# Layer 1 of a two-layer diffusion backbone: VectorE and ScalarE in program order, V projected two token tiles to a PSUM bank, output transposes of two tiles in one PSUM unit

## The chip, the core and the metric

The kernel runs on one core of one Trainium2 chip. A core has five engines with an instruction queue each: TensorE (PE: matmuls and transposes; PEld is its weight load), VectorE (DVE), ScalarE (ACT), GpSimd (POOL) and SyncE (SP, which issues DMA transfers). The metric is the time of the whole program on the device in microseconds. Lower is better.

## The reference

Two layers run over 1024 latent tokens of width 1024 and 256 context tokens. Layer 0 is multi-head latent attention, layer 1 differential attention. Both end in a gated output projection, a residual sum and a layer norm. The change touches layer 1 alone. It has 8 heads; a head has two query and two key maps of width 64 and one value of width 128:

```python
q, k, v, gate = jnp.split(t @ w_in, 4, axis=-1)
q, k = apply_rope(q, cos, sin), apply_rope(k, cos, sin)      # latent tokens only
o1 = softmax(q[..., 0] @ k_all[..., 0] * scale) @ v_all      # keys: latent and context tokens
o2 = softmax(q[..., 1] @ k_all[..., 1] * scale) @ v_all
o = rms_norm(o1 - lam_full * o2, g_sub) * (1.0 - lambda_init)
x = layer_norm(ALPHA * x + gate_x * ((o * silu(gate)) @ out_w), ln_g, ln_b)
```

The context stream of layer 1 is needed for its keys and values only, since layer 1 is the last.

## The kernel before

Activations of layer 1 lie transposed in SBUF as two fp16 halves, h1H and h1L (high part and rest), for 10 tiles of 128 tokens: tiles 0 to 7 latent, 8 and 9 context. Each product is three matmuls, high by high, low by high and high by low (`mm3`, L184 to L187). Splitting a value costs one ScalarE operation for the high part and one VectorE operation for the rest (`split`, `split16`, L175 to L182).

PSUM in layer 1 has two units of three banks (tag `s`, 1536 numbers a partition) for attention and two single banks (tag `b`) for projections. A new tile takes a buffer whose last user has been read; the instruction that writes first waits for that reader.

Attention of head h and token tile t is a step of `step1`, written out in TensorE's order:

- scores of map 0 into a unit (6 matmuls); on VectorE the row maximum (L1151), on ScalarE the exponential (L1152)
- a slot of side work, 3400 units of cost (`SLOT1`; a matmul of 512 columns costs 512)
- values of tile t-2 (30 matmuls, L1173 to L1175) and scores of map 1, both into the other unit; maximum and exponential; on ScalarE the copy of the values' result and its squares (L1179, L1180)
- a slot of 4300
- ten transposes of tile t-1 (L1167) into the unit that held scores 0, and their split into ph (ScalarE, L181) and pl (VectorE, L182)
- a slot of 6800
- on VectorE the combine of the two maps of tile t (L1154 to L1156)

The side work of head h is the projection of head h+1: K in chunks of 512, 512 and 256 tokens (`prod_k1`), Q in two of 512 (`prod_q1`), each with a rope on VectorE (L1048, L1049) and GpSimd (L1050, L1051), then V and the gate (`prod_v1`): the 256 context tokens transposed, then one bank for each token tile, emptied by ScalarE copies into Vf and gg (L1122, L1124). `prod_w` prepares a head's weights in stages: load, two squares (L979), a small matmul for the norm (L982) with its scale on VectorE and GpSimd, and two splits. `weave` starts its stages at the numbers of main yields in `WAT`. Closing work of K, Q and V (splits, the gate's SiLU with two table loads) is kept in `later` and run at the end of a step.

`tc.manual_schedule(engines=...)` names the engines whose instructions keep the program's order. In both layers that is TensorE (`MAN = 'P'`, `MAN1 = 'P'`). The order on the others is chosen by the framework's scheduler. `HP` sets its priority and is 0.

Head 7 has no projection beside it. `out_open` loads the rest of out_w (four weights, L1213, scaled by L1215, split by L176 and L177); from step 2 on the side work is the output projection of tile t-2 (`out_tile1`), with transposes by `out_turn`: seven blocks of the next tile in one unit, woven in by `out_turns`, and the tile's own last block in another, since head 7 gives it late (L1256).

Of the kernel before, what the change touches and what calls it, by code (L numbers as in the profile page):

```python
# [17 lines left out]
P = 128  # L18
D = 1024
KT = D // P  # L20
SEQ = 1024
# [10 lines left out]
H1, HD = 8, 64  # L32
LAMBDA_INIT = 0.8 - 0.6 * math.exp(-0.3 * 1)
PB = (3, 4)
WAT = ((6, 14, 21, 27, 34), (3, 10, 18, 25, 32))
NOW = 4
MAN = 'P'
MAN1 = 'P'
HP = 0
LAG = 2  # L40
CHUNKS = ((0, 512), (512, 512), (1024, 256))
# [12 lines left out]
def hybrid_kernel(  # L54
# [95 lines left out]
    idn = fv(idr)  # L150
# [132 lines left out]
    def pow2_of(scale, unscale, amax, target, g):  # L283
        dve.tensor_scalar(g[:, 0:1].bitcast(I32), amax.bitcast(I32), 0x7F800000, None, op0=ALU.bitwise_and)
        dve.reciprocal(g[:, 1:2], g[:, 0:1])
        dve.tensor_scalar_mul(scale, g[:, 1:2], target)
        dve.tensor_scalar_mul(unscale, g[:, 0:1], 1.0 / target)
# [669 lines left out]
    def w1(tag):  # L957
        sh, d, b = TAG1[tag]
        return rot(place[tag], sh, d, tag, b)
# [8 lines left out]
    def prod_w(h, which, bank_=lambda: bank("b"), load=sp):  # L968


        wt[which] = []
        ws, sq = [], w1("sq")
        for q in range(2):
            ws.append(w1("ws"))
            load.dma_start(ws[q], dw[q * 512:(q + 1) * 512, h, which * 256:(which + 1) * 256].rearrange(
                "(k p) c -> p k c", p=P))
        yield 0
        for q in range(2):
            act.activation(w1("wsq"), ws[q].rearrange("p a b -> p (a b)"), AF.Square, accum_out=sq[:, q:q + 1])  # L979
        yield 0  # L980
        bk = bank_()
        pe.matmul(bk[:, :2], ones, sq, start=True, stop=True)  # L982
        u, p2 = w1("uw"), w1("uw")
        dve.tensor_reduce(u[:, 0:1], bk[:, :2], axis=AX.X, op=ALU.add)
        pool.tensor_scalar(u[:, 0:1], u[:, 0:1], 1.01, 1e-30, op0=ALU.mult, op1=ALU.add)
        pool.tensor_tensor(u[:, 0:1], u[:, 0:1], poshalf, op=ALU.pow)
        pow2_of(u[:, 1:2], u[:, 0:1], u[:, 0:1], 16384.0, p2)

        dve.tensor_tensor(u[:, 0:1], u[:, 0:1], hun, op=ALU.mult)
        if which:  # L990
            us1[h] = w1("us")
            pool.tensor_tensor(us1[h], u[:, 0:1], vic, op=ALU.mult)
        else:
            es1[h] = w1("es")
            dve.tensor_scalar(es1[h], u[:, 0:1], u[:, 0:1], hic, op0=ALU.mult, op1=ALU.mult)
        un[which] = u[:, 0:1]
        yield 0
        for q in range(2):
            wH, wL = w1("wH"), w1("wL")
            split16(wH, wL, ws[q], u[:, 1:2])  # L1000
            wt[which] += [(wH[:, j, :], wL[:, j, :]) for j in range(4)]
            yield 0
# [97 lines left out]
    def prod_v1(h):  # L1100
        w, uv = wt[1], un[1]
        gg, Vf = w1("gg"), w1("Vf")
        vt[h] = vh, vl = w1("vh"), w1("vl")
        vT = w1("rr")[:, :CTX]
        ps = bank("b")
        for k in range(KT):
            mm3(ps[:, :CTX], w[k][0][:, :P], w[k][1][:, :P], h1H[:, k, SEQ:], h1L[:, k, SEQ:], k == 0, k == KT - 1)
            if k % 2:
                yield 6 * CTX
        act.copy(vT, ps[:, :CTX])  # L1110
        for t in (0, 1, 2, 8, 3, 4, 9, 5, 6, 7):
            ts = slice(t * P, (t + 1) * P)
            ps = bank("b")
            if t < 8:
                for k in range(KT):
                    mm3(ps[:, :256], h1H[:, k, ts], h1L[:, k, ts], *w[k], k == 0, k == KT - 1)
                    if k % 2:
                        yield 6 * 276
            else:
                pe.transpose(ps[:, :P], vT[:, (t - 8) * P:(t - 7) * P], idn)  # L1120
                yield 256
            act.copy(Vf[:, t, :], ps[:, :P])  # L1122
            if t < 8:
                act.copy(gg[:, t, :], ps[:, P:256])  # L1124

        def top():
            split16(vh, vl, Vf, kc1)
            g = gg.rearrange("p t d -> p (t d)")
            act.activation(g, g, AF.Silu, scale=uv)
            sp.dma_start(sg_d[1][:SEQ, h * P:(h + 1) * P].rearrange("(t p) d -> p t d", p=P), gg)  # L1130

        later.append(top)
        yield 0
# [111 lines left out]

    oT = {}

    def out_turn(t, k0, n):

        o, _ = og[t]  # L1250
        if k0 == 0:
            oT[t] = w1("tH"), w1("tL")
        tH, tL = oT[t]
        tb = unit()
        for j in range(n):
            pe.transpose(tb[:, j * P:(j + 1) * P], o[:, (k0 + j) * P:(k0 + j + 1) * P], idn)  # L1256
        f = lambda x: x[:, k0:k0 + n, :].rearrange("p a b -> p (a b)")
        split(f(tH), f(tL), tb[:, :n * P])

    def out_turns(t):  # L1260
        if t >= SEQ // P:
            return
        out_turn(t, 0, KT - 1)
        yield 1792

    def out_tile1(t):

        ts = slice(t * P, (t + 1) * P)
        tH, tL = oT[t]
        res = w1("res")  # L1270
        sp.dma_start(res, zn_d[ts, :])
        y = [bank("b") for _ in range(2)]

        def mm(hh, k):
            c = slice(hh * 512, hh * 512 + 512)
            mm3(y[hh], tH[:, k, :], tL[:, k, :], oHL[k][0][:, c], oHL[k][1][:, c], k == 0, k == KT - 1)

        for hh in range(2):
            for k in range(KT - 1):
                mm(hh, k)  # L1280
                yield 1600
                if hh == 1 and k == 3:
                    out_turn(t, KT - 1, 1)
                    yield 256
        z, bs = w1("z"), w1("bs")
        for hh in range(2):
            mm(hh, KT - 1)
            c = slice(hh * 512, hh * 512 + 512)
            dve.tensor_tensor(z[:, c], y[hh], res[:, c], op=ALU.add)  # L1289
            dve.bn_stats(bs[:, hh, :], z[:, c])  # L1290
        yield 3200
        mv = w1("mv")
        dve.bn_aggr(mv[:, 0:2], bs)
        rstd_of(mv[:, 2:3], mv[:, 1:2], 1.0, 1)
        if t == SEQ // P - 1:
            for hh in range(2):
# [25 lines left out]
    with tc.manual_schedule(engines={ENG[c] for c in MAN1}):  # L1322
# [37 lines left out]
        for h in range(H1):  # L1360
            last = h == H1 - 1
            if not last:
                G = chain(weave(weave(chain(prod_k1(h + 1), prod_q1(h + 1, 0), prod_q1(h + 1, 1)), part(), (1, 9, 17, 25)),
                                prod_w(h + 1, 1), WAT[0]),
                          weave(prod_v1(h + 1), prod_w(h + 2, 0) if h + 2 < H1 else
                                chain(*[out_w1(k, lambda: w1("ws").rearrange("p a b -> p (a b)")) for k in range(NOW)]),
                                WAT[1] if h + 2 < H1 else range(1, 40, 4)))
            else:
                while later:
                    later.pop(0)()  # L1370
                out_open()
            for t in range(SEQ // P):
                if last:
                    if t >= 2:
                        out_load(t)
                    G = weave(out_tile1(t - 2), out_turns(t - 1), (9, 12)) if t >= 2 else iter(())
                    if t == 2:
                        G = chain(out_turns(0), G)
                    credit[0] = 0
                step1((h, t), G, SLOT1 if not last else SLOTO)  # L1380
                if last:
                    for _ in G:
                        pass
            for _ in G:
                pass
        for t in range(SEQ // P - 2, SEQ // P):
            G = weave(out_tile1(t), out_turns(t + 1), (9, 12))
            credit[0] = 0
            step1(None, G, SLOTO)
            for _ in G:  # L1390
                pass
# [74 lines left out]
```

## Time and profile before

| what | value |
|---|---|
| three runs | 1897.23, 1899.69, 1902.23 us; median 1899.69 |
| profiled execution | 1893.88 us |
| its span, first to last instruction | 1891.8 us |
| mean granted TensorE clock | 0.967 |
| layer 1, opening projections | about 972 to 1029 us of the span |
| layer 1, heads 0 to 6 | about 1029 to 1703 us |
| layer 1, head 7 and output | about 1703 to 1892 us |

In the rows of the profile, L716 is line 716 of the kernel before. "a<-b" names what is written and read, without buffer numbers. A group gives its count, busy time and mean; a wait row gives the waiting engine, tile and line, what released it, then the total, the count and the longest. A timeline row gives start, duration, engine, line, operation and, in brackets, the engine's idle time before it with its releaser. Rows of stretches give start and end, length, busy time of PE, PEld, DVE, ACT and POOL with their instruction counts, granted clock, DMA share and GB/s. Matmuls are pipelined, so the next one starts before the shown duration is over; the pace is read from starts.

### The profile page before, as it was taken

Reading aid. Unit: us, or ns where it says so; the run is one execution under the profiler, and the core shown is the slowest. Engines: PE = TensorE matmul, PEld = TensorE weight load, DVE = VectorE, ACT = ScalarE, POOL = GpSimd, SP = SyncE. Lnnn points to the kernel's source line nnn. Section 1 sums busy time; section 2 is a strip of 40 time slices with the busy share of each in tenths; the row PEclk is TensorE's granted clock in tenths of the full one; section 3 lists DMA queues with packets and bytes.
Section 4 is the critical chain, followed back from the end, with each engine's and each line's share of the span. In section 5 each row is a group of like instructions: output and inputs, shape, how many; then the busy total and the mean of one; then the engine's idle time right before and its main releaser. Section 6 shows DMA issues by size and latency. Waiting matters only on the chain. (4 is left out here: it accounts for less than half of the span.)

```text
span 1891.8 us, 35302 instructions
## 1 busy us (share of the span) xinstructions
PE 1696.9 (90%) x14468; PEld 1236.6 (65%) x14468; DVE 1193.3 (63%) x1552; ACT 1001.2 (53%) x1495; POOL 853.9 (45%) x741
## 2 busy tenths in 40 slices
PE   7898989999999998788878898999999999896997
PEld 4888965656666665466646575757575767574775
DVE  6546865575665658337754667776766676866663
ACT  3442157867777778611124464655665665655341
POOL 1443036767776677656641214132323232525453
PEclk8999999999999999989989999999999999997999
DMA  8246630110111013143334222121212121204331
GB/s 289 75 131 184 181 102 19 37 46 24 39 43 46 21 44 108 51 165 133 106 109 114 65 59 65 51 74 52 64 41 63 42 64 52 59 23 156 117 97 58
DMA packets 111214, 154.75 MB, mean 82 GB/s; under 512 B 13415, under 2 KB 84679, under 8 KB 111054
## 3 DMA queue, kind: packets, MB, share of 16 engines
q1 hardware_dynamic: 104238, 146.22, 26.0%
q10 hardware_dynamic: 6816, 6.29, 1.0%
q8 instruction: 114, 1.87, 0.4%
q14 instruction: 46, 0.38, 0.1%
HBM read 98.65 MB, written 27.07 MB: 66 GB/s over the span
## 5 line engine op out<-in xcount | busy, mean ns | idle before, releaser
L716 POOL TENSOR_TENSOR pl<-p,ph 128x1024 f16<-128x1024 f32 (+1 forms) x176 | 363.8, 2073 | 148.5 <-ACT ph L715 122.1
L1152 ACT ACTIVATE p<-ps_s,mx 128x1280 f32<-128x1280 f32 x128 | 169.7, 1326 | 176.2 <-DVE mx L1151 175.9
L696 DVE TENSOR_REDUCE mx<-ps_a 128x1 f32<-128x1024 f32 x128 | 155.5, 1222 | 134.1 <-PE ps_a L694 134.1
L714 ACT ACTIVATE p<-ps_a,esc 128x1024 f32<-128x1024 f32 (+1 forms) x176 | 189.0, 1074 | 96.4 <-PE ps_a L772 89.9
L1151 DVE TENSOR_REDUCE mx<-ps_s 128x1 f32<-128x1280 f32 x128 | 189.4, 1485 | 72.9 <-PE ps_s L1145 71.9
L715 ACT CAST ph<-p 128x1024 f16<-128x1024 f32 (+1 forms) x176 | 177.1, 1006 | 5.5
L1178 POOL TENSOR_TENSOR sm<-sm,us 128x1 f32<-128x1 f32 x64 | 19.1, 299 | 339.2 <-DVE sm L1154 339.1
L785 PE MATMUL ps_d<-Vh,pl 128*128 128x65 f16 x1344 | 145.9, 194 | 5.5 <-POOL pl L716 5.4
L782 PE MATMUL ps_d<-Vh,ph 128*128 128x65 f16 x1344 | 148.0, 195 | 0.0
L1144 PE MATMUL ps_s<-KS,QS 128*128 128x512 f16 (+1 forms) x384 | 133.7, 348 | 15.6 <-DVE pl L182 7.8
L784 PE MATMUL ps_d<-Vl,ph 128*128 128x64 f16 x1344 | 146.8, 193 | 0.0
L185 PE MATMUL ps_b<-wH,h1H 128*128 128x256 f16 x512 | 140.9, 275 | 5.0 <-ACT gg L1124 2.5
L186 PE MATMUL ps_b<-wL,h1H 128*128 128x256 f16 x512 | 140.9, 275 | 0.0
L187 PE MATMUL ps_b<-wH,h1L 128*128 128x256 f16 x512 | 140.9, 275 | 0.0
L185 PE MATMUL ps_b<-h1H,wH 128*128 128x512 f16 (+1 forms) x384 | 132.9, 346 | 6.1 <-ACT wH L181 6.1
L782 PEld LDWEIGHTS <-ph 128*128 128x128 f16 x1344 | 123.2, 97 | 18.1 <-issue 4.8
L187 PE MATMUL ps_b<-h1H,wL 128*128 128x512 f16 (+1 forms) x384 | 132.7, 345 | 0.8 <-DVE wL L182 0.8
L186 PE MATMUL ps_b<-h1L,wH 128*128 128x512 f16 (+1 forms) x384 | 132.8, 346 | 0.0
L784 PEld LDWEIGHTS <-ph 128*128 128x128 f16 x1344 | 123.9, 98 | 11.9
L1173 PE MATMUL ps_s<-vh,ph 128*128 128x128 f16 x640 | 113.3, 222 | 19.3 <-DVE pl L182 14.9
L770 PE MATMUL ps_a<-qH,KH 100*128 100x512 f16 x320 | 122.5, 383 | 8.7 <-ACT p L714 4.8
L785 PEld LDWEIGHTS <-pl 128*128 128x128 f16 x1344 | 123.1, 97 | 7.1 <-POOL pl L716 7.1
(367 smaller groups left out, 4970.5 us busy)
## 6 DMA issues: line engine op xcount, KB each, us to landing
ws<-in_dw SPq DMA_DIRECT2D x30, 512.0 KB, 4.0
adw<-in_ada_w SPq DMA_DIRECT2D x24, 512.0 KB, 4.8
g<-sg_d SPq DMA_DIRECT2D x18, 512.0 KB, 3.6
adaw<-in_ada_w SPq DMA_DIRECT2D x16, 512.0 KB, 7.2
sg_d<-gg ACTq DMA_DIRECT2D x40, 128.0 KB, 3.4
o<-o_d SPq DMA_DIRECT2D x10, 512.0 KB, 3.9
o_d<-op SPq DMA_DIRECT2D x7, 640.0 KB, 3.7
xt<-in_xT SPq DMA_DIRECT2D x16, 256.0 KB, 3.6
```

The lines of the kernel that those rows point to most:

```text
L185: pe.matmul(ps, aH, bH, start=start, stop=False, skip_group_check=skip)
L186: pe.matmul(ps, aH, bL, start=False, stop=False, skip_group_check=skip)
L187: pe.matmul(ps, aL, bH, start=False, stop=stop, skip_group_check=skip)
L696: dve.tensor_reduce(mx[:, t, 0:1], ps, axis=AX.X, op=ALU.max)
L714: act.activation(p32[:, :n], st, AF.Exp, scale=esc0)
L715: act.copy(ph[:, :n], p32[:, :n])
L716: pool.tensor_tensor(pl[:, :n], p32[:, :n], ph[:, :n], op=ALU.subtract)
L782: pe.matmul(pv[:, t, :], ph[:, ts], Vh[:, k, h, :], start=(k == kcs[0] and t == 0), stop=False, skip_group_check=True)
L784: pe.matmul(pv[:, t, :V0], ph[:, ts], Vl[:, k, h, :], start=False, stop=False, skip_group_check=True)
L785: pe.matmul(pv[:, t, :], pl[:, ts], Vh[:, k, h, :], start=False, stop=(k == NT - 1), skip_group_check=True)
L1151: dve.tensor_reduce(mx[:, m:m + 1], u[:, :NTOK], axis=AX.X, op=ALU.max, negate=True)
L1152: act.activation(p[m], u[:, :NTOK], AF.Exp, bias=mx[:, m:m + 1], accum_out=sm[:, m:m + 1])
```

## The change

`MAN1` becomes `'PDA'`: VectorE and ScalarE keep the program's order in layer 1 too. `prod_w` yields once more, between the norm's GpSimd operations and the scale, and `WAT` gets a sixth number, with some moved. V's token tiles go two to a bank, in the order 0-1, 2-3, the context pair 8-9, 4-5, 6-7, each bank emptied by two copies of 256 columns (the context pair by one). `out_turn` takes a list of parts: the own last block of tile t and seven blocks of tile t+1 go into one unit, at the second product of the second half in place of the fourth, and `out_turns` and its weaving go.

```diff
-WAT = ((6, 14, 21, 27, 34), (3, 10, 18, 25, 32))
+WAT = ((6, 14, 21, 24, 28, 34), (3, 10, 18, 21, 25, 32))
...
-MAN1 = 'P'
+MAN1 = 'PDA'
...
         pool.tensor_tensor(u[:, 0:1], u[:, 0:1], poshalf, op=ALU.pow)
+        yield 0
         pow2_of(u[:, 1:2], u[:, 0:1], u[:, 0:1], 16384.0, p2)
...
-        for t in (0, 1, 2, 8, 3, 4, 9, 5, 6, 7):
-            ts = slice(t * P, (t + 1) * P)
+        for i, t0 in enumerate((0, 2, 8, 4, 6)):
             ps = bank("b")
...
+            for j in range(2):
+                t = t0 + j
+                ts = slice(t * P, (t + 1) * P)
+                if t < 8:
+                    for k in range(KT):
+                        mm3(ps[:, j * 256:(j + 1) * 256], h1H[:, k, ts], h1L[:, k, ts], *w[k], k == 0, k == KT - 1)
+                        if k % 2:
+                            yield 6 * 276
+                else:
+                    pe.transpose(ps[:, j * P:(j + 1) * P], vT[:, (t - 8) * P:(t - 7) * P], idn)
+                    yield 256
+            if t0 < 8:
+                src = ps.rearrange("p (t c) -> p t c", t=2)
+                act.copy(Vf[:, t0:t0 + 2, :], src[:, :, :P])
+                act.copy(gg[:, t0:t0 + 2, :], src[:, :, P:])
             else:
...
-            act.copy(Vf[:, t, :], ps[:, :P])
-            if t < 8:
-                act.copy(gg[:, t, :], ps[:, P:256])
+                act.copy(Vf[:, t0:t0 + 2, :], ps[:, :2 * P].rearrange("p (t c) -> p t c", t=2))
...
-    def out_turn(t, k0, n):
+    def out_turn(parts):
+        u = unit()
+        c0 = 0
+        for t, k0, n in parts:
+            o, _ = og[t]
+            if k0 == 0:
+                oT[t] = w1("tH"), w1("tL")
+            for j in range(n):
+                pe.transpose(u[:, c0 + j * P:c0 + (j + 1) * P], o[:, (k0 + j) * P:(k0 + j + 1) * P], idn)
+            c0 += n * P
...
+            split(f(oT[t][0]), f(oT[t][1]), u[:, c0:c0 + n * P])
...
-                if hh == 1 and k == 3:
-                    out_turn(t, KT - 1, 1)
-                    yield 256
+                if hh == 1 and k == 1:
+                    out_turn([(t, KT - 1, 1)] + ([(t + 1, 0, KT - 1)] if t + 1 < SEQ // P else []))
+                    yield 2000
...
-                    G = weave(out_tile1(t - 2), out_turns(t - 1), (9, 12)) if t >= 2 else iter(())
+                    G = out_tile1(t - 2) if t >= 2 else iter(())
                     if t == 2:
-                        G = chain(out_turns(0), G)
+                        out_turn([(0, 0, KT - 1)])
```

More of the change, by code (lines that the diff above doesn't have):

```diff
@@ L1110, in prod_v1 @@
         act.copy(vT, ps[:, :CTX])
-        for t in (0, 1, 2, 8, 3, 4, 9, 5, 6, 7):
-            ts = slice(t * P, (t + 1) * P)
+        for i, t0 in enumerate((0, 2, 8, 4, 6)):
             ps = bank("b")
-            if t < 8:
[L1115 to L1118, printed above, removed]
-            else:
-                pe.transpose(ps[:, :P], vT[:, (t - 8) * P:(t - 7) * P], idn)
-                yield 256
-            act.copy(Vf[:, t, :], ps[:, :P])
-            if t < 8:
-                act.copy(gg[:, t, :], ps[:, P:256])
+            for j in range(2):
[13 more added lines that the diff above has]
+                act.copy(gg[:, t0:t0 + 2, :], src[:, :, P:])
+            else:
+                act.copy(Vf[:, t0:t0 + 2, :], ps[:, :2 * P].rearrange("p (t c) -> p t c", t=2))
         def top():
@@ L1246, in hybrid_kernel @@
     oT = {}
-    def out_turn(t, k0, n):
[L1250 to L1264, printed above, removed]
+    def out_turn(parts):
[8 more added lines that the diff above has]
+            c0 += n * P
+        c0 = 0
+        for t, k0, n in parts:
+            f = lambda x: x[:, k0:k0 + n, :].rearrange("p a b -> p (a b)")
+            split(f(oT[t][0]), f(oT[t][1]), u[:, c0:c0 + n * P])
+            c0 += n * P
     def out_tile1(t):
@@ L1281, in out_tile1 @@
                 yield 1600
-                if hh == 1 and k == 3:
-                    out_turn(t, KT - 1, 1)
-                    yield 256
+                if hh == 1 and k == 1:
+                    out_turn([(t, KT - 1, 1)] + ([(t + 1, 0, KT - 1)] if t + 1 < SEQ // P else []))
+                    yield 2000
         z, bs = w1("z"), w1("bs")
@@ L1386, in hybrid_kernel @@
         for t in range(SEQ // P - 2, SEQ // P):
-            G = weave(out_tile1(t), out_turns(t + 1), (9, 12))
+            G = out_tile1(t)
             credit[0] = 0
```

## The prediction

> **What bounds the kernel now.** I read the page's first lines, then the busy time of the three stretches in which the edited code runs, then who made TensorE wait in them, then one step row by row.
>
> ```profile
> span 1891.8 us, 35302 instructions
> PE 1696.9 (90%) x14468; PEld 1236.6 (65%) x14468; DVE 1193.3 (63%) x1552; ACT 1001.2 (53%) x1495; POOL 853.9 (45%) x741
> ```
> ```profile
> core 0: us, PE busy (x) PEld busy (x) DVE busy (x) ACT busy (x) POOL busy (x), PEclk, DMA share, GB/s
> 972.40:1029.10 56.70, 52.22 (x343) 34.57 (x344) 22.52 (x51) 18.16 (x38) 12.38 (x14) 0.92 0.34 96
> 1029.10:1702.90 673.80, 620.12 (x5241) 450.06 (x5239) 467.89 (x573) 395.88 (x703) 202.21 (x308) 1.00 0.21 56
> 1702.90:1891.80 188.90, 152.21 (x936) 117.25 (x933) 111.02 (x124) 68.16 (x104) 91.23 (x82) 0.90 0.32 107
> ```
>
> The rows are the opening projections, heads 0 to 6, and the last head with the output. TensorE is the bound: in heads 0 to 6 it is busy 620.1 of 673.8 us, 11.07 us for each of the 56 steps, and idle 53.7 us, 7.7 us a head. VectorE and ScalarE have a third of their time free, so what matters is not how much they do but when. Program order on them could win the 53.7 us at most, plus what TensorE waits in the other two rows. The largest waits in heads 0 to 6:
>
> ```profile
> PE ps_s L1173 <- DVE pl L182: 14.3, 13, 1.7
> PE ps_s L1167 <- ACT p L1152: 10.0, 9, 2.1
> PE ps_b L982 <- DVE kr L1049: 4.9, 7, 0.8
> PE ps_s L1167 <- DVE p L1156: 4.8, 4, 1.5
> PE ps_s L1144 <- ACT o L1179: 4.6, 3, 1.5
> PE ps_b L185 <- ACT gg L1124: 1.3, 7, 0.2
> ```
>
> No wait is longer than 2.1 us in these rows. One step shows the chain and its order (start, duration, engine):
>
> ```profile
> 1435.96 0.38 PE L185 MATMUL ps_b<-h1H,wH 128*128 128x512 f16 x1
> 1436.16 1.49 DVE L1151 TENSOR_REDUCE mx<-ps_s 128x1 f32<-128x1280 f32 x1 [2.56 <-PE ps_s L1145]
> ...
> 1437.68 1.33 ACT L1152 ACTIVATE p<-ps_s,mx 128x1280 f32<-128x1280 f32 x1 [2.63 <-DVE mx L1151]
> 1437.90 1.26 PE L1167 MATMUL ps_s<-idr,p 128*128 128x128 f32 x10
> ...
> 1439.00 0.36 ACT L1179 ACTIVATE o<-ps_s,sm 128x128 f32<-128x128 f32 x1
> 1439.13 0.17 DVE L1154 RECIPROCAL sm<-sm 128x2 f32<-128x2 f32 x1 [1.49 <-ACT p L1152]
> ...
> 1439.45 0.31 ACT L1180 ACTIVATE o<-o 128x128 f32<-128x128 f32 x1
> 1439.62 1.55 DVE L1156 SCALAR_TENSOR_TENSOR p<-p,sm,p 128x1280 f32<-128x1280 f32 x1
> ...
> 1439.76 1.31 ACT L181 ACTIVATE ph<-ps_s,lcf 128x1280 f16<-128x1280 f32 x1
> ...
> 1441.09 0.73 DVE L1048 STREAM_SHUFFLE rsw<-ps_b 128x512 f32<-128x512 f32 x1
> ...
> 1441.72 0.67 DVE L1049 TENSOR_TENSOR kr<-ps_b,cosB 128x512 f32<-128x512 f32 x1
> 1442.31 1.54 DVE L182 SCALAR_TENSOR_TENSOR pl<-ps_s,lcf,ph 128x1280 f16<-128x1280 f32 x1
> 1442.44 0.38 PE L982 MATMUL ps_b<-sq,ones 128*128 128x2 f32 x2 [0.68 <-DVE kr L1049]
> ```
>
> VectorE's order here is maximum, combine (L1156), rope (L1048, L1049), then pl: the scheduler fills the wait for ph with the combine and the rope. TensorE's L982, the small matmul of the weight norm, sits in the bank that the rope empties, and waits only 0.68 us.
>
> **The change, part by part.** I put the changed program's instruction order on each engine beside this. TensorE's order in the heads is the same but for V's banks.
>
> *VectorE in program order.* In every step it is now maximum 0, maximum 1, pl of the tile before, rope, combine. pl needs ph, and ph stands on ScalarE behind the second exponential, the output copy and its square. From the end of the second scores: 1.49 + 1.32 + 0.45 + 0.31 + 1.31 = 4.9 us (starts from row to row), so VectorE stands idle from 1.5 to 4.9 us in a step, and rope, combine and the next maximum all queue behind. After pl (1.47, like the combine from start to start), the combine (0.49 for its two small operations, then 1.47) and the next maximum (1.49), 9.8 us of the 11.07 are gone; the step has room for about 1 us of other VectorE work there. What exceeds it makes the next maximum late, then the exponential, then TensorE's transposes, which reuse that PSUM unit.
>
> *Squares ahead of ph.* In the second step of each head both squares (L979) stand in the program before ph:
>
> ```profile
> L979 ACT ACTIVATE wsq<-ws x24: 1042/1057/1095, 1032.3 to 1595.2; 128x1024 f32<-128x1024 f32 x24
> L1122 ACT COPY Vf<-ps_b x70: 245/265/293, 1033.4 to 1699.4; 128x128 f32<-128x128 f32 x70
> 1446.89 2.19 ACT L181 ACTIVATE wH<-ws,uw 128x1024 f16<-128x1024 f32 x2
> 1448.08 2.48 DVE L182 SCALAR_TENSOR_TENSOR wL<-ws,uw,wH 128x1024 f16<-128x1024 f32 x2 [1.15 <-ACT wH L181]
> 1450.48 1.55 DVE L182 SCALAR_TENSOR_TENSOR kL<-kr,kc,kH 128x1280 f16<-128x1280 f32 x1
> ```
>
> Then L982 needs: 4.9 + 2.1 (two squares) + 1.47 (pl) + 0.63 + 0.67 (rope) = 9.8 us after the second scores. TensorE reaches L982 at 1442.44 - 0.68 = 1441.76, 5.8 us after them, with projections and transposes of its own. It waits 4.0 us, or 4.6 with lateness inherited from the step before, where 0.68 stands now. Behind L982 wait the next scores and all that follows. The loads that the squares read are issued by SyncE, whose order stays the scheduler's, two or more steps ahead, so I cost them at nothing; late, one adds up to 5.2 us to the same chain, the longest such wait before:
>
> ```profile
> ACT wsq L979 <- DMA ws<-in_dw: 44.8, 19, 5.2
> ```
>
> *The step after it* carries, between pl and the next maximum, a rope (1.25), half of the wL row (1.24), combine, kL (1.55) and the short kL (at most half of that, 0.75); ahead of ph on ScalarE stands half of the wH row (1.09). Chain from second scores to the next step's exponential: 1.49 + 1.32 + 0.76 + 1.09 + 1.31 + 1.47 + 1.25 + 1.24 + 1.94 + 1.55 + 0.75 + 1.49 + 1.32 = 17.0 us. TensorE reaches the transposes after one step and one slot, 11.07 + 1.94 = 13.0. Wait 4.0; 4.4 in my walk of a whole head with these durations. The step behind it has rope and short kL in that place: 1.49 + 1.32 + 0.76 + 1.31 + 1.47 + 1.25 + 1.94 + 0.75 + 1.49 + 1.32 = 13.1, wait 0.1, or 1.8 with the lateness that it inherits. A head's first step has half of wH's row ahead of ph and vl (1.54, as pl) behind the combine: 13.7, wait 0.7, or 1.6.
>
> *V two tiles to a bank.* It takes out 7 of 17 small ScalarE copies a head; one is 0.27 us, so a 256-wide copy is between 0.27 and 0.53, I take 0.33. ScalarE saves 1 to 2 us a head, beside TensorE: nothing on the path. But tiles 4,5 use the bank of tiles 2,3 (the context pair, 8,9, takes the other bank, which the norm's tiny result has just left). Tiles 2,3 end with a step; their copies stand in program order behind the next step's exponential 0. TensorE runs scores 0, two transposes (0.22), then waits for maximum 1.49, exponential 1.33 and copies 0.66, less the 0.22: 3.3 us at least; with maximum 0 about 2 us late behind pl and combine, 5.1. The like wait before (L185 on gg) is 0.2.
>
> So a head waits 1.6 + 4.6 + 4.4 + 1.8 + 5.1 and some 0.7 in small ones, 18.2 us, against 7.7: +10.5. The retimed prod_w (an added yield, weights split 7 yields apart) is in these orders. Heads 0 to 3 also run two gate products on VectorE (of wL's size, 1.24), one of them behind pl: +1.2 each; head 4's two gate matmuls wait on a rope like L982, some 1.5 more. Heads 0 to 6: 73.5 + 5 + 1.5 = +80 us. With no inherited lateness, the lower bound: (0.7 + 4.0 + 4.0 + 0.1 + 3.3) - 7.7 = +4.4 a head, +31.
>
> *Opening projections.* No attention runs here; V's pairs halve the evictions:
>
> ```profile
> PE ps_b L185 <- DVE rr L1049: 2.3, 1, 2.3
> PE ps_b L185 <- ACT gg L1124: 1.2, 3, 0.5
> ```
>
> I take -3 us, bounds -3.5 and +2 (a pair's two copies in its bank).
>
> *Last head.* Per tile, output transposes now take one PSUM unit in place of two; the second one waited for pl:
>
> ```profile
> 1710.01 1.31 PE L1167 MATMUL ps_s<-idr,p 128*128 128x128 f32 x10 [2.42 <-ACT p L1152]
> ...
> 1738.38 0.80 PE L187 MATMUL ps_b<-oH,tL 128*128 128x512 f32 x1 [5.96 <-DVE tL L177]
> ```
> ```profile
> PE ps_s L1256 <- DVE pl L182: 10.2, 6, 1.8
> ```
> ```profile
> 1720.00:1725.00 5.00, 3.28 (x18) 1.92 (x16) 2.78 (x3) 1.69 (x2) 2.09 (x1) 0.80 1.02 406
> ```
>
> That wait goes: -10 us. The last tile's own block is turned two products earlier and so waits longer for its normalised output: +1. Against it, at the head's start the four out_w products (L1215) and their ScalarE casts, which need loads, now stand ahead of the first maximum and exponential. The DMA engines are full (1.02) until 1725, so exponential 0 comes near 1729 and the transposes at 1710.01 slip by 20 us. The 5.96 and other waits up to 1738 are then mostly gone; I give back 10 (all of 15 to 20 and 5 bound it): +10.
>
> **Sum** against the profiled execution's 1893.88 us (span and 2.1 around it): +80 - 3 - 10 + 1 + 10 = +78, 1972. I add 5 for clock lost after the long waits (next paragraph): +83. The three runs' median, 1899.69, lies 5.8 above that execution; from it, 1983.
>
> **The clock.**
>
> ```profile
> 1284.15 1.12 PE L1167 MATMUL ps_s<-idr,p 128*128 128x128 f32 x8 [1.88 <-ACT p L1152]
> ```
> ```profile
> 1285.00:1290.00 5.00, 5.00 (x31) 3.68 (x30) 3.42 (x4) 2.69 (x8) 2.70 (x4) 0.66 0.17 41
> ```
>
> Right after a wait of 1.88 us the granted clock of the next 5 us is 0.66; 0.34 of 5 us is 1.7 us lost. Three waits of 4 to 5 us in each of 7 heads, all followed by such a loss: 36 us. Most of it may hide in the next wait, hence the 5. [...]
>
> **Rivals.** (1) *Short chains* (0.20): the five waits come at their lower bounds, +31 - 3 - 10 + 1 + 10 = +29, 1929. For it: each bound is a sum of rows. Against: nothing in program order lets VectorE catch up between them. (2) *Clock* (0.17): the whole 36 us is paid beside the waits, 1899.7 + 78 + 36 = 2014. (3) *Faster* (0.11): pl ahead of rope and combine takes the two largest waits of heads 0 to 6 away (14.3 and 10.0), the small ones follow, and the new chains hide. Then 1899.7 - 53.7 - 3 - 10 = 1833 at best, 1866 with half. It decides if the waits of a head stay under 7.7 us; the pl row of the list speaks for it, the 9.8 against 5.8 us at L982 against. (4) *No change* (0.04): new waits replace old ones one for one, 1900.
>
> **How the numbers follow.** The forecast has 0.48: 1955 to 2005 by itself. The range reaches down to rival 1 and up to rival 2: 1925 to 2020, leaving out rivals 3 and 4 and little more. Slower 0.85, within 0.3% (what a measurement can tell from no change) 0.04, faster 0.11.
>
> **What would show it.** L982 waiting 4 to 5 us on the rope in each head; L185 waiting 4 to 5 us on gg once a head; L1167 waiting about 4 us on the exponential once a head; VectorE idle before pl in most steps, about 3 us, released by ph; a stretch of about 20 us without transposes at the last head's start, VectorE waiting on out_w's DMA; no wait of the output transposes on pl. Heads 0 to 6 should take 745 to 760 us. I am wrong if no wait of heads 0 to 6 exceeds 2.5 us.

## The result and the profile after

The changed kernel takes 2050.05 us (median of 4 runs, 2048.04 to 2055.37) against 1898.46 for the kernel before: ratio 1.0817, interval 1.076 to 1.0874. The direction was forecast, the size was not: 1983 us was the forecast, 1925 to 2020 its range.

The first lines of the page and the three stretches, cut at the same events as before (first product of the opening projections, first scores of head 0, first scores of head 7). Line numbers are those of the changed kernel: scores L1150 and L1151, maximum L1157, exponential L1158, transposes L1173, values L1179 to L1181, combine L1160 to L1162, rope L1049 to L1052, output turns L1263.

```profile
span 2053.6 us, 35202 instructions
PE 1739.1 (85%) x14468; PEld 1261.9 (61%) x14468; DVE 1223.8 (60%) x1552; ACT 995.3 (48%) x1423; POOL 867.3 (42%) x741
```
```profile
974.20:1025.50 51.30, 49.95 (x342) 33.63 (x343) 20.46 (x49) 15.27 (x25) 13.64 (x14) 0.95 0.32 88
1025.50:1846.00 820.50, 667.21 (x5241) 477.86 (x5239) 507.49 (x572) 392.96 (x644) 215.78 (x309) 0.91 0.17 47
1846.00:2053.60 207.60, 150.25 (x936) 116.56 (x933) 105.73 (x126) 68.10 (x105) 89.23 (x82) 0.89 0.29 98
```

The span grew by 161.8 us: 146.7 in heads 0 to 6 (820.5 against 673.8), 18.7 in the last head (207.6 against 188.9); the opening projections are 5.4 shorter (51.3 against 56.7) and begin 1.8 later. In heads 0 to 6 two things happened. TensorE waits 153.3 us in place of 53.7, +99.6. And the same 5241 matmul records take 667.2 us in place of 620.1, +47.1: the granted clock is 0.91, not 1.00.

TensorE's waits in heads 0 to 6 of the changed kernel, which add up to 153.2 of the 153.3 us:

```profile
PE ps_s L1173 <- ACT p L1158: 87.0, 24, 9.3
PE ps_b L185 <- ACT gg L1128: 35.0, 7, 6.4
PE ps_b L982 <- DVE kr L1050: 25.7, 7, 4.5
PE ps_s L1179 <- DVE pl L182: 2.9, 13, 0.3
PE ps_b L1212 <- DVE kr L1050: 2.6, 1, 2.6
```

The three forecast places are there and little else (5.5 us): the norm's matmul on the rope, the V bank on gg, the transposes on the exponential. The first two have the forecast size, 3.7 and 5.0 us a head (forecast 4.6 and 5.1). The transposes have 12.4 a head where 1.6 + 4.4 + 1.8 = 7.8 was forecast, and their longest wait is 9.3 where 4.4 was. VectorE in the step of that wait, row by row:

```profile
1176.92 1.49 DVE L1157 TENSOR_REDUCE mx<-ps_s 128x1 f32<-128x1280 f32 x1 [1.96 <-PE ps_s L1151]
1181.63 1.38 DVE L182 SCALAR_TENSOR_TENSOR wL<-ws,uw,wH 128x1024 f16<-128x1024 f32 x1 [3.22 <-ACT wH L181]
1182.93 1.54 DVE L182 SCALAR_TENSOR_TENSOR pl<-ps_s,lcf,ph 128x1280 f16<-128x1280 f32 x1
...
1185.62 1.95 DVE L182 SCALAR_TENSOR_TENSOR wL<-ws,uw,wH 128x1024 f16<-128x1024 f32 x1
...
1187.68 1.03 DVE L1161 SCALAR_TENSOR_TENSOR sm<-sm,nlam 128x1 f32<-128x1 f32 x1
1188.75 1.55 DVE L1162 SCALAR_TENSOR_TENSOR p<-p,sm,p 128x1280 f32<-128x1280 f32 x1
1190.22 1.54 DVE L182 SCALAR_TENSOR_TENSOR kL<-kr,kc,kH 128x1280 f16<-128x1280 f32 x1
1195.27 0.75 DVE L182 SCALAR_TENSOR_TENSOR kL<-rr,es,kH 128x512 f16<-128x512 f32 x1 [3.51 <-DMA KS<-kL]
1195.94 2.88 DVE L1157 TENSOR_REDUCE mx<-ps_s 128x1 f32<-128x1280 f32 x2
```

This is the chain that was forecast at 17.0 us from second scores to the next exponential's end. It took 21.9 (1176.92 to 1197.46, where that exponential starts, and its 1.33). The operations are the forecast ones, and two things are added. Before the short kL, VectorE stands 3.51 us: Q's low half goes into the one buffer that holds K's, and waits until the DMA has read that. And L1161 and the second wL take 1.03 and 1.95 us.

The last head's first maximum stands behind the four out_w products, as forecast:

```profile
1862.58 1.90 DVE L1221 SCALAR_TENSOR_TENSOR z<-z,gsub,gate 128x1024 f32<-128x1024 f32 x1 [11.06 <-DMA z<-in_out_w]
...
1875.29 2.88 DVE L1157 TENSOR_REDUCE mx<-ps_s 128x1 f32<-128x1280 f32 x2
```
```profile
PE ps_s L1173 <- ACT p L1158: 30.0, 2, 28.1
PE ps_s L1263 <- DVE o L1191: 13.1, 7, 2.9
```

The first row of these waits is the start, 28.1 us where some 20 were forecast. The second was not forecast: the output turns no longer wait on pl, but on o, the last head's normalised block.

### The profile page after: what moved, and what is told of

It is laid out like the page before. It is cut to its first block, busy times and chain, and to the rows that moved or that the text cites. A ratio compares the mean times of both kernels' runs of the same rounds, so it can differ in the third digit from the quotient of the medians.

```text
span 2053.6 us, 35202 instructions
## 1 busy us (share of the span) xinstructions
PE 1739.1 (85%) x14468; PEld 1261.9 (61%) x14468; DVE 1223.8 (60%) x1552; ACT 995.3 (48%) x1423; POOL 867.3 (42%) x741
## 5 line engine op out<-in xcount | busy, mean ns | idle before, releaser
L1158 ACT ACTIVATE p<-ps_s,mx 128x1280 f32<-128x1280 f32 x128 | 169.9, 1328 | 345.5 <-DVE mx L1157 345.5
L1157 DVE TENSOR_REDUCE mx<-ps_s 128x1 f32<-128x1280 f32 x128 | 186.3, 1482 | 72.8 <-PE ps_s L1151 72.8
L159 POOL TENSOR_SCALAR ss<-ss 128x1 f32<-128x1 f32 x64 | 12.2, 190 | 446.8 <-ACT o L1186 446.3
L1173 PE MATMUL ps_s<-idr,p 128*128 128x128 f32 x640 | 92.6, 298 | 117.0 <-ACT p L1158 117.0
L182 DVE SCALAR_TENSOR_TENSOR pl<-ps_s,lcf,ph 128x1280 f16<-128x1280 f32 x64 | 99.0, 1546 | 153.2 <-ACT ph L181 153.2
L1173 PEld LDWEIGHTS ps_s<-idr,p 128*128 128x128 f32 x640 | 79.2, 153 | 132.2 <-ACT p L1158 129.3
L185 PE MATMUL ps_b<-h1H,wH 128*128 128x512 f16 (+1 forms) x384 | 142.0, 370 | 6.1 <-ACT wH L181 6.1
L186 PE MATMUL ps_b<-h1L,wH 128*128 128x512 f16 (+1 forms) x384 | 141.0, 367 | 0.0
L187 PE MATMUL ps_b<-h1H,wL 128*128 128x512 f16 (+1 forms) x384 | 139.8, 364 | 0.8 <-DVE wL L182 0.8
L1150 PE MATMUL ps_s<-KS,QS 128*128 128x512 f16 (+1 forms) x384 | 136.3, 355 | 2.2 <-DVE pl L182 2.2
```

Of the source, the lines that this page charges most:

```text
L185: pe.matmul(ps, aH, bH, start=start, stop=False, skip_group_check=skip)
L186: pe.matmul(ps, aH, bL, start=False, stop=False, skip_group_check=skip)
L187: pe.matmul(ps, aL, bH, start=False, stop=stop, skip_group_check=skip)
L1157: dve.tensor_reduce(mx[:, m:m + 1], u[:, :NTOK], axis=AX.X, op=ALU.max, negate=True)
L1158: act.activation(p[m], u[:, :NTOK], AF.Exp, bias=mx[:, m:m + 1], accum_out=sm[:, m:m + 1])
L1173: pe.transpose(u[:, j * P:(j + 1) * P], pc[:, j * P:(j + 1) * P], idn)
```

## The experiments

Each ran beside the kernel before on the same chip; a ratio is to that, with its interval. Waits are TensorE's, in heads 0 to 6 where nothing else is said. The diffs leave unchanged lines out.

### Which part of the change: four switches

Without the order, the order alone, and the order on one engine:

```diff
e1_order_off     -MAN1 = 'PDA'   +MAN1 = 'P'      (changed kernel)
e2_order_only    -MAN1 = 'P'     +MAN1 = 'PDA'    (kernel before)
e3_vector_only   -MAN1 = 'PDA'   +MAN1 = 'PD'     (changed kernel)
e4_scalar_only   -MAN1 = 'PDA'   +MAN1 = 'PA'     (changed kernel)
```

> The changed kernel with VectorE and ScalarE given back to the scheduler in layer 1; the two V tiles to a bank, the merged output turns and the spread weight preparation stay. Theory: the order alone made the loss, and the other parts are worth little or a gain: 1885 to 1900 us, heads 0 to 6 about 675 us, no wait over 2.5 us in them, output turns 5 to 10 us cheaper than before. Rival: the two V tiles to a bank cost by themselves, 5 us of wait in each of 7 heads and the half clock behind it: 1940 us or more, with the wait of L185 on gg still there.

> The kernel before with VectorE and ScalarE of layer 1 in program order, nothing else. Theory: the waits of the transposes on the exponential and of the norm's matmul on the rope are all there (some 110 us of idle time in heads 0 to 6, and half-clock stretches behind each), the wait of 35 us on the V bank is not: 2000 us, 1980 to 2025. Rival: one V tile to a bank puts as many evictions behind the exponential as two, and the wait stays: 2045 us or more.

> The changed kernel with VectorE alone in program order, ScalarE the scheduler's. Theory (both orders share the loss: VectorE's queue behind pl, ScalarE's evictions behind the exponential): the V bank's wait goes, the waits of the transposes stay: 1960 to 2000 us. Rival (VectorE's order is the whole loss): 2035 us or more. Other rival (ScalarE's order is): under 1920.

> The changed kernel with ScalarE alone in program order, VectorE the scheduler's. Theory (shared): the V bank's wait of 5 us a head stays, the waits of the transposes on the exponential mostly go: 1930 to 1960 us. Rival (VectorE's order is the whole loss): 1900 or less. Other rival (ScalarE's order is): 2000 or more.

Measured: without the order 1903.72 us, ratio 1.0063 (1.0038 to 1.0089); the order alone 2060.27, 1.088 (1.0847 to 1.0913); VectorE's alone 1963.9, 1.0379 (1.0342 to 1.0417); ScalarE's alone 1975.52, 1.0442 (1.0404 to 1.0481). The order is the whole loss: the kernel before with it is as slow as the changed one. The rest of the change is slightly slower where a gain was expected. With the scheduler's order (e1) heads 0 to 6 take 681.6 us against 673.8 before, and the last head, of which more below, 194.5 against 188.9. In the heads the scores wait longer for ScalarE's copy of the values' result, 22.7 us where it was 4.6:

```profile
PE ps_s L1150 <- ACT o L1185: 22.7, 10, 2.8
```

This comes from V's pairs or from the spread weight preparation, which were not tried apart.

The second kernel's waits, then those of VectorE's order alone, then of ScalarE's:

```profile
PE ps_s L1167 <- ACT p L1152: 89.2, 24, 9.6
PE ps_b L185 <- ACT gg L1124: 34.9, 14, 3.0
PE ps_b L982 <- DVE kr L1049: 25.7, 7, 4.5
```
```profile
PE ps_s L1173 <- ACT p L1158: 74.6, 22, 8.9
PE ps_b L982 <- DVE kr L1050: 9.5, 6, 2.2
```
```profile
PE ps_b L185 <- ACT gg L1128: 34.6, 7, 6.1
PE ps_s L1173 <- ACT p L1158: 31.9, 14, 4.9
```

With one V tile to a bank the wait on gg is there in the same size, 14 times 2.5 us in place of 7 times 5.0: e2's rival held. So it is ScalarE's order that makes it, and the pairs only gather it. The waits on the exponential are mostly VectorE's: 74.6 us with its order alone, 31.9 with ScalarE's alone. The wait on the rope needs both: 9.5 us with VectorE's order alone, 4.6 with ScalarE's, 25.7 with both. The theory's numbers held for VectorE alone; ScalarE alone came out 15 us above them. In heads 0 to 6 the two orders cost 45.6 and 52.8 us alone (727.2 and 734.4 in place of e1's 681.6) and 138.9 together, more than their sum.

### What a wait costs: V's evictions ahead of the yield

The V loop yields after its last product, and the generator is resumed in the next slot, behind the next step's exponential; only then do the copies enter the program. Moved:

```diff
-                        if k % 2:
+                        if k % 2 and (j == 0 or k < KT - 1):
                             yield 6 * 276
...
                 act.copy(gg[:, t0:t0 + 2, :], src[:, :, P:])
+                yield 6 * 276
```

> The changed kernel, but the two evictions of a V bank stand in the program right behind the bank's last product, ahead of the next exponential, not behind it; TensorE's order is the same. Theory: the wait of L185 on gg (35.0 us in 7 times) goes with the half-clock stretch of 6.8 us behind each; a half-clock stretch costs about 0.3 of its length, so some 14 us more: 2000 us, 1990 to 2010. Rival (clock lost behind a wait is hidden in the next wait): the 35 us alone, 2015 us. Other rival (the evictions now hold the exponential up, and the transposes wait instead): 2035 or more.

Measured: 1998.1 us, ratio 1.0518 (1.0485 to 1.0552). The stretch of heads 0 to 6 and its waits:

```profile
1026.60:1794.10 767.50, 648.30 (x5241) 465.11 (x5239) 507.37 (x572) 394.46 (x644) 216.22 (x310) 0.93 0.18 50
```
```profile
PE ps_s L1174 <- ACT p L1159: 86.0, 25, 9.3
```

The wait on gg is gone, idle time fell by 34.1 us (153.3 to 119.2) and TensorE's busy time for the same matmuls by 18.9 (667.2 to 648.3). The theory held in both halves: a wait of this length cost its own time and about half as much again in clock. The clock around two waits of the changed kernel shows how, the transposes' wait that ends at 1198.93 and the V bank's that ends at 1233.51:

```profile
1181.00:1194.30 13.30, 8.59 (x64) 4.81 (x62) 10.06 (x10) 4.82 (x5) 4.62 (x5) 1.00 0.48 133
1194.30:1204.54 10.24, 5.61 (x21) 3.65 (x22) 5.37 (x6) 4.80 (x8) 1.37 (x3) 0.50 0.25 59
...
1231.85:1238.67 6.82, 5.16 (x37) 4.41 (x37) 0.56 (x4) 1.88 (x5) 0.00 (x0) 0.50 0.00 0
```

The granted clock is 0.50 for 10.24 and for 6.82 us, and 1.00 ahead of them. Each stretch begins within the wait and goes on for some 5 us after it, over the next scores and products.

### The order of the combine, the rope and pl

The scheduler had combine, rope, pl. First (e7) the combine alone ahead of pl; then (e8) with it V's evictions as above and the rope written right behind its projection, ahead of the yield; then (e9) in the changed kernel pl's VectorE half behind the third slot and the combine; then (e10) that with V's evictions, the late out_w products and the late turns of the sections below.

```diff
e7_combine_first
             some(side, at[1])
+            was = joined.pop(0) if joined else None
+            if cur:
+                joined.append((cur, *next(S)))
...
-            if cur:
-                joined.append((cur, *next(S)))
e8_three_orders      (K's rope; Q's and V's evictions alike)
-            for ps in proj1(n, c0, slice(P, 2 * P)):
-                yield 3 * n
-            if c0 < SEQ:
-                rope1(ps[:, :n], n, ...)
+            for ps, done in proj1(n, c0, slice(P, 2 * P)):
+                if done and c0 < SEQ:
+                    rope1(ps[:, :n], n, ...)
+                yield 3 * n
e9_pl_last
-        split16(ph, pl, u[:, :NTOK]..., lcf[:, 0:1])
+        act.activation(ph, src, AF.Copy, scale=lcf[:, 0:1])
+        return lambda: dve.scalar_tensor_tensor(pl, src, lcf[:, 0:1], ph, ...)
...
                     joined.append((cur, *next(S)))
+            if low:
+                low()
```

> The changed kernel with the combine ahead of pl in VectorE's order, as the scheduler had it; TensorE's order is the same. Theory: VectorE is idle for 3 us or more ahead of pl, the combine fits there, and the next maximum comes 1.9 us earlier in every late step: the 87 us that the transposes wait fall to about 55, the half-clock share with them, 2010 us, 1995 to 2025. The waits on the rope (25.7) and on gg (35.0) stay. Rival: the combine itself waits for the second exponential and holds pl back by as much: 2040 or more.

> The changed kernel with three pieces moved in program order: V's evictions right behind their product, the combine ahead of pl, and the rope right behind its projection, so ahead of pl where it was behind; TensorE's order is the same. Theory: the waits on gg and on the rope go, those of the transposes are halved, and the clock comes back with them: heads 0 to 6 about 700 us, 1930 us, 1910 to 1955; what is left is the start of the last head (28 us). Rival: program order can't be had for nothing wherever the pieces stand, since each waits behind another: 1975 or more.

> The changed kernel with pl's VectorE half behind the third slot's projections and the combine, so that rope, combine, pl is again the order, all of it by hand; ScalarE as changed, TensorE's order the same. Theory: TensorE finishes the projection behind the transposes, so only a pl behind that slot lets the rope go first; the wait of L982 on the rope falls from 25.7 us to 6 or less, the transposes lose a part of theirs, the wait on gg stays at some 30: 2005 us, 1990 to 2020. Rival: pl that comes later holds the values and the unit instead, by as much: 2035 or more.

> The kernel of the run before, with V's evictions right behind their product, the last head's four output weight products behind its second step in place of ahead of its first, and the merged turns two products later. Theory: the five places are what program order lost, and each goes by itself: 50 us for V's evictions, some 20 for the start of the last head, some 8 for the turns: 1930 us, 1910 to 1950. Rival: 1890 to 1905, as with the scheduler, if the order by hand has no other weak place. Other rival: 1965 or more, if waits taken away in one place come back in the next.

Measured: 2028.97 us, 1.0704 (1.0671 to 1.0738); 1986.54, 1.0457 (1.043 to 1.0484); 2070.61, 1.0911 (1.0883 to 1.0939); 2015.53, 1.0624 (1.0599 to 1.0648). All four miss their theory. The first lies between its theory and its rival; the second and the third have their rival's time, the fourth that of its second rival. The waits of the first, of the second, of the third:

```profile
PE ps_s L1173 <- ACT p L1158: 56.3, 8, 7.9
PE ps_s L1179 <- DVE pl L182: 31.9, 19, 2.2
```
```profile
PE ps_s L1181 <- DVE pl L182: 33.2, 19, 2.2
PE ps_b L982 <- DVE kr L1050: 30.6, 7, 4.5
```
```profile
PE ps_s L1181 <- DVE pl L1176: 110.9, 39, 6.0
PE ps_b L982 <- ACT wsq L979: 1.4, 5, 0.3
```

The combine ahead of pl takes the transposes' waits from 87.0 to 56.3, as expected, and gives that back in the values' unit, which now waits on pl (2.9 to 31.9): the combine itself waits for the second exponential. The rope can't be had ahead of pl by writing it early, since in TensorE's order its projection ends behind the transposes that pl reads; the 30.6 us stay. With pl behind that slot they go, to 1.4, and that part of e9 is as expected; but then the values wait for pl 39 times. One of the longest of these waits, in e9:

```profile
1182.05 1.94 DVE L182 SCALAR_TENSOR_TENSOR wL<-ws,uw,wH 128x1024 f16<-128x1024 f32 x1
...
1186.63 1.54 DVE L1176 SCALAR_TENSOR_TENSOR pl<-ps_s,lcf,ph 128x1280 f16<-128x1280 f32 x1
...
1188.32 0.27 PE L1181 MATMUL ps_s<-vh,ph 128*128 128x128 f16 x1 [6.00 <-DVE pl L1176]
```

ScalarE had finished ph, pl's last input, at 1180.70. A rope, the weights' low half and the combine stand ahead of pl in VectorE's queue, and TensorE waits 6.00 us for what it could have had earlier. With the other three places mended as well (e10) this wait is still 114.8 us, in 45 times.

### The longest wait: Q's split and the place of the splits

Open at this point was whether the 9.3 us belong to the DMA that holds K's buffer, to the splits' place ahead of the maximum, or to the queue as a whole.

```diff
e13_q_split_buffer
+"qL": ([P, 512], F16, 1)
-            H, L = w1("kH")[:, :n], w1("kL")[:, :n]
+            H, L = w1("kH")[:, :n], w1("qL")
e14_splits_later     (from the end of step1 to behind the second maximum)
                 next(V, None)
+            for _ in range(len(later)):
+                later.pop(0)()
             some(side, at[1])
...
-            for _ in range(len(later)):
-                later.pop(0)()
```

> The changed kernel with a buffer of its own for the low half of Q's split, which shared one with K's. Theory: the longest wait of a head, 9.3 us, holds 3.5 us in which VectorE stands at that short product until the DMA has read K's half out of the buffer (23.4 us in 7 times), with the next maximum behind it; some 2.7 us of it go (its other operand comes from ScalarE), the wait falls to about 6.6 and the half-clock stretch with it: 2026 us, 2018 to 2035. Rival: VectorE's queue is late there with or without the DMA, and the next steps wait instead: 2042 or more.

> The changed kernel with K's, Q's and V's splits, which stood ahead of the next step's first maximum, behind that step's second maximum; buffers as they were. Theory: the maxima pass 1.55 + 0.75 + 3.5 us of VectorE's work and DMA wait, and the splits fall into the 3 us in which VectorE waits for ph: the 9.3 us fall to about 3.5, 41 us in all and some 12 of clock: 1997 us, 1985 to 2015. Rival: the DMA wait now stands ahead of pl, and the values and scores wait for it: 2025 or more.

Measured: 2026.87 us, ratio 1.0701 (1.0667 to 1.0735), and 2047.14, 1.0811 (1.0776 to 1.0846). Waits of the first, then of the second with one of VectorE's own:

```profile
PE ps_s L1173 <- ACT p L1158: 71.6, 26, 6.9
```
```profile
PE ps_s L1173 <- ACT p L1158: 44.6, 17, 3.8
PE ps_s L1179 <- DVE pl L182: 26.6, 30, 2.3
DVE kL L182 <- ACT kH L181: 63.1, 21, 3.4
```

The buffer is a cause of its own, in the expected size: the longest wait is 6.9, and 23 us of the kernel go with 2.4 us a head; e13's theory held. Moving the splits takes the transposes' waits down to 44.6 with a longest of 3.8, as expected, and wins nothing: VectorE stands at the splits in the new place (63.1 us) with pl behind, and the values wait. TensorE's idle time in heads 0 to 6 does fall, from 153.3 to 141.1 us, but its busy time grows from 667.2 to 673.8: there are 27 stretches at half clock in place of 23. The time is the rival's, though VectorE no longer waits for the DMA that the rival named.

### The last head: out_w's products and the merged turns

```diff
e11_out_w_late       (the four products behind step 1 of head 7)
+                    if t == 1:
+                        out_rest()
e6_late_turn         (on the changed kernel with MAN1 = 'P')
e12_before_merged_late   (on the kernel before, out_turn alone)
-                if hh == 1 and k == 1:
+                if hh == 1 and k == 3:
                     out_turn([(t, KT - 1, 1)] + ...)
```

> The changed kernel with the last head's four output weight products (L1221 and their casts) behind its second step, not ahead of its first. Theory: the 28.1 us that the first transposes wait are VectorE and ScalarE standing at those products while their loads land; they go, and with them most of the 27 us at half clock: last head 185 us in place of 207.6, 2027 us, 2020 to 2035. Rival: the loads land no sooner, and the third step waits as long: last head 202 or more, 2045 or more.

> The changed kernel with VectorE and ScalarE the scheduler's, and the merged output turns two products later, where the last block's turns stood before. Theory: the 17.5 us that the merged turns wait for the last head's block o, against 10.2 us on pl before, come from their place, and go: last head 180 us against 194.6 with the turns as changed, 1888 us (0.995 of before). Rival: the block is late wherever the turns stand within the tile, since a single unit of PSUM now holds both: last head 190 or more, ratio 1.002 or more.

> The kernel before with one thing changed: the output turns of two tiles in one PSUM unit, at the place where the last block's turns stood. Order, V banks and weight preparation are as before. Theory: the 10 us that the output turns waited on pl go, and heads 0 to 6 stay at 674 us: 1882 us, ratio 0.988 to 0.994. Rival: the gain of the late turns depended on the V banks or the weight preparation: ratio 0.997 or more.

Measured: 2039.8 us, ratio 1.075 (1.0726 to 1.0774); 1888.84, 0.9955 (0.9934 to 0.9977); 1885.47, 0.9937 (0.9914 to 0.996). The last head of e11, of e1 (turns as changed, scheduler's order) and of e12:

```profile
1843.00:2033.80 190.80, 148.44 (x936) 114.91 (x933) 102.09 (x126) 68.13 (x105) 88.52 (x82) 0.93 0.32 106
```
```profile
1707.40:1901.90 194.50, 155.26 (x936) 120.63 (x933) 112.03 (x124) 68.55 (x105) 90.82 (x82) 0.90 0.31 104
```
```profile
1704.80:1884.50 179.70, 150.09 (x936) 116.87 (x934) 112.76 (x124) 68.31 (x105) 90.87 (x82) 0.92 0.34 113
```

With the products behind the second step the last head is 16.8 us shorter in the profiled executions (207.6 to 190.8), where some 23 were expected: that is what the start costs. By the medians the whole kernel won 10.3, which leaves it just above the theory's 2035. One wait of 8.4 us is new, on the split of the output turns, which stands behind out_w's casts on ScalarE. The merged turns cost 5.6 us where the change put them (188.9 to 194.5) and win 9.2 two products later (179.7), when o is nearer to ready. The theories of e6 and e12 held. The fastest kernel here is the last, with the merged turns at that place and nothing else of the change; its lead over e6 is within the two intervals.

### Do the gains add up

V's evictions, Q's buffer, the splits' place, out_w's products and the late turns in one kernel, still in program order on both engines.

> The changed kernel with five places put right together: V's evictions right behind their product, the low half of Q's split in its own buffer, the splits behind the next step's maxima, the output weight products behind the last head's second step, the merged turns two products later; VectorE and ScalarE still in program order. Theory (the long waits are separate and add up, 52 + 50 + 10 + 13 us): 1925 us, 1905 to 1945; what is left over the kernel before is the rope behind pl and the small waits. Rival (a wait taken out comes back in the next place): 1960 or more. If 1890 or less, program order by hand is as good as the scheduler's.

Measured: 1965.93 us, ratio 1.0393 (1.0351 to 1.0436), 84 us under the changed kernel. One by one the five had given 52.0, 23.2, 2.9, 10.3 and 14.9 (the last as e6 against e1), 103 in all. Four fifths of that came (some seven tenths if one goes by the ratios), and this is the rival's time. Left in heads 0 to 6:

```profile
PE ps_s L1174 <- ACT p L1159: 51.0, 22, 3.8
PE ps_s L1180 <- DVE pl L182: 26.9, 25, 2.4
PE ps_b L982 <- DVE kr L1050: 22.9, 7, 4.4
```

## Why the prediction was right in kind and too small

| term of the sum | forecast, us | measured, us |
|---|---|---|
| waits in heads 0 to 6 | +80 | +99.6 |
| clock | +5 | +47.1 |
| opening projections | -3 | -5.4, of which 3.0 in waits |
| last head, start | +10 | +17 (e11) |
| last head, output turns | -10 and +1 | +6 (e1 against before) |
| last head, all | +1 | +18.7 |

*The clock is the step that failed most.* The prediction worked out 36 us for 21 long waits and took 5, because "most of it may hide in the next wait". The price of a wait was about right: 47.1 us over 23 stretches at half clock is 2.0 each. The hiding was the error: e5 took 7 waits away and got 34.1 us of idle time and 18.9 of busy time. A likely reason is that what stands behind a wait is the next scores, products and transposes, and these set when the next wait begins. Rival 2, with 36, was nearest on this term. With 47 in place of 5, and nothing else mended, the forecast would have been 2025.

*The turn of the next step was mis-sized.* Its chain of 17.0 us took 21.9: 3.5 for a DMA that still reads the shared split buffer, which the prediction had not looked for and so put at nothing, and the rest mostly for two VectorE operations that ran beside GpSimd's rope and took longer, L1161 with 1.03 us and the second wL with 1.95 (means before: 0.24 and 1.28). The wait went from 4.4 to 9.3, the same 4.9. Seven times 4.9 is 34 us, which covers the 32 by which the transposes' 87.0 exceed the 54.6 that 7.8 a head gave them. e13 shows the buffer's part; the slower operations were not tried alone.

*L982 and the V bank were right*, 25.7 and 35.0 us against 32 and 36. The mechanism at L982 is shown by e9, where pl behind the rope takes the wait to 1.4, and by e3, where the scheduler's ScalarE takes it to 9.5. On the V bank the prediction named the reuse by tiles 4 and 5; the place of the copies behind the exponential, which it also named, was enough by itself (e2, e5).

*The last head failed in two terms.* The start costs 17 and not 10: the transposes slipped by 28 us, not 20. The merged turns were priced by the wait that they remove (10.2 us on pl, which did go), with 1 us for the tile's own block; but the block now holds up the whole unit, seven blocks of the next tile included, and TensorE waits 13.1 us for it. e6 and e12 show that the place, not the merging, is at fault. Taken apart, the start and the turns cost 16.8 and 5.6 us, 22.4; together they came to 18.7.

*The opening projections* gained more than the bound of 3.5 us. The forecast waits, on gg and the rope, fell from 3.5 to 0.5. The rest is TensorE's busy time, 52.2 to 50.0, with a granted clock of 0.95 where it was 0.92; no term stood for that, and its cause stays open.

Not settled is whether any order by hand would match the scheduler's here. e9, e10, e14 and e15 show that taking one wait out of an in-order queue often hands it to the next instruction; the best of those tried with both engines in program order (e15) leaves 3.9%.

## What to carry to other kernels

Before an engine is put in program order, walk its queue once and write down for each instruction the last thing that it needs, a DMA that still reads its output buffer included: whatever stands behind a late one is late too, even with its own inputs there (in e9 pl started 5.9 us after ph was done). In generators that interleave work, an eviction written behind the last yield enters the queue one slot later than its product; writing it ahead of the yield was worth 52 us here. And price a long TensorE wait at more than its own length. Of the 25 waits of 2.5 us and more in heads 0 to 6 of the changed kernel 23 have a stretch at half clock beside them. Such a stretch cost about 2 us: in the changed kernel, e5, e13 and e14 the matmuls of heads 0 to 6 took 47.1, 28.2, 39.9 and 53.7 us longer than in the kernel before, over 23, 16, 23 and 27 stretches at half clock, 1.7 to 2.0 us each. The loss hardly grew with the wait: in the two stretches shown above, around waits of 9.3 and 4.8 us, TensorE was busy for 5.61 and 5.16 us.

## What the runs showed of the hardware that was not expected

*The clock fell around some waits of 2.6 to 2.8 us, and not around others.* In heads 0 to 6 of the changed kernel the granted clock is 0.50 for 3.4 to 10.2 us around each of the 18 waits of 3.8 us and more, around 5 of the 7 between 2.5 and 2.9, and around none of the 8 between 1.3 and 2.2. Of three waits of 2.82 us at L982 the first, which ends at 1167.76, has a stretch of 6.8 us, the other two have none. In the kernel before the forecast had one case in heads 0 to 6, the wait of 1.88 us with a clock of 0.66 behind it; a wait of 2.43 us there, which ends at 1040.29, has none, with 1.00 from 1036 to 1048. So the length of a wait does not settle it alone; what else does was not shown.

*L1161, L1162 and wL took longer beside GpSimd's rope.* Heads 0 to 6, before and then after:

```profile
L1156 DVE SCALAR_TENSOR_TENSOR p<-p,sm,p 128x1280 f32<-128x1280 f32 x56 | 86.8, 1550 | 1.6
L1155 DVE SCALAR_TENSOR_TENSOR sm<-sm,nlam 128x1 f32<-128x1 f32 x56 | 13.4, 239 | 1.7
```
```profile
L1162 DVE SCALAR_TENSOR_TENSOR p<-p,sm,p 128x1280 f32<-128x1280 f32 x55 | 98.9, 1799 | 1.9
L1161 DVE SCALAR_TENSOR_TENSOR sm<-sm,nlam 128x1 f32<-128x1 f32 x55 | 29.6, 538 | 2.0
```
```profile
1186.56 2.13 POOL L1052 TENSOR_TENSOR rr<-rr,rsw 128x512 f32<-128x512 f32 x1
```

A VectorE operation on one number a partition went from 239 to 538 ns on average; the one of 1.03 us above starts within this GpSimd row and ends as it does. Of L1161's 55 rows the 28 beside the rope (L1051, L1052) took 0.84 us on average and up to 1.32, the other 27 at most 0.26; of L1162's the 13 beside it took 2.44 to 2.64, all others 1.55 or 1.56; of wL's the 7 beside it took 1.94 or 1.95, the others 1.38 to 1.40. pl took 1.54 or 1.55 in both kernels, also in the 20 rows of the kernel before that ran beside the rope. In the new order the combine comes right behind the rope, and so beside GpSimd's half of it; before, one row of L1155 and none of L1156 ran beside it. It goes with VectorE's order: L1161 takes 487 ns with that order alone (e3), 254 and 245 with the scheduler's (e1, e4).
